# A gated delta-rule scan: block inversion over 16x16 blocks, decay mask on GpSimd, SiLU taken directly

## The chip, the cores and the metric

The kernel runs on one core of a Trainium2 chip. The time is the device time of one execution in microseconds (us); beside it stands one execution recorded by the hardware profiler. The engines are named as in the profile: PE (TensorE, with its weight loads as PEld), DVE (VectorE), ACT (ScalarE), POOL (GpSimd) and SP (SyncE, which only issues transfers).

## The reference

A backbone of two layers over 256 context tokens and 512 latent tokens, width 1024, in float32. Layer 0 joins a differential attention with a bidirectional gated DeltaNet; layer 1 joins a linear recurrence with windowed attention; each has a gated convolutional feed-forward part. Only the DeltaNet of layer 0 is touched. Cut to what matters:

```python
qkv = jax.nn.silu(_dwconv(qkv, conv_w))            # then q, k, v
qb = _l2norm(qb); kb = _l2norm(kb)
g = -exp(a_log) * softplus(a_raw + dt_bias); beta = sigmoid(b_raw)
# per chunk and direction
G = cumsum(g); decay = where(i >= j, exp(G_i - G_j), 0)
t_mat = where(i > j, beta_i * (k k^T) * decay, 0) + I
u = solve(t_mat, beta * v); w = solve(t_mat, beta * exp(G) * k)
v_new = u - w s;  o = (q exp(G)) s + (q k^T * decay) v_new
s = s * exp(G_last) + (k exp(G_last - G))^T v_new
```

## The kernel before

**Layout.** Activations lie with features on the 128 partitions and all 768 tokens on the free axis. The kernel is written in a tile framework: the program gives the work in order, and a planner, working from its own cost estimates, lays down before the run the order in which each engine executes its instructions, puts in the semaphores and shares buffers. Each engine then runs its queue strictly in that order.

**Projections.** `proj` loads one 1024x128 weight tile, splits it into a rounded high part (ACT, L333) and a low remainder (L335, two in three on DVE, one on POOL) and runs 48 matmuls of 128x384 for it (L346, L347, L349), called `pj` in the rows. Two PSUM accumulators hold them in turn.

**q and k.** `gdn_proj` adds a four-tap convolution (one ACT copy, six DVE instructions, L435) and the SiLU as y(1 + tanh(y/2)), which is twice the SiLU: a tanh on ACT (L964) and a product on DVE (L965). The factor 2 is taken out later. `gdn_qk` squares the result on ACT (L983), sums squares by a matmul with ones (L986), copies them out (L987), and forms the inverse root by Ln and Exp over all four heads at once. v goes the same way (`gdn_v`), with a transpose instead of the norm.

**The scan.** There are 6 chunks of 128 tokens and 8 problems (4 heads in 2 directions) in each. For chunk s, four functions:

- `gdn_prep`: two transfers put the rows of G across all partitions (tile A); eight DVE instructions subtract the column of G plus log-beta and add the causal mask (L804); one Exp over 128x1024 (L805); k k^T (L811) times it gives LT (L812); the four 32x32 diagonal blocks of LT are copied by ACT into LTd (L816); q k^T (L821) is multiplied onto A (L823).
- `gdn_inv`: the 32x32 diagonal blocks are inverted on DVE. A transpose spreads LTd (L831); then for each row i from 1 to 31 a product (L839) and a reduce (L840), each needing the row before; two transposes (L842, L844) give the inverse Xd and its transpose XTd.
- `gdn_merge`: two doubling levels on TensorE (L862, L869, L871, then L880, L885), with copies by ACT and DVE between, join the 32x32 inverses into 64x64 and 128x128 ones.
- `gdn_step`: applies the inverse to v, forms the output and updates the state (L903 to L952). L903 is POOL's product of q with exp(G), and L1046 are POOL's issues of loads for the attention that follows.

**Order.** k, then q, then `gdn_prep` of chunks 0 and 1 and `gdn_inv` of chunk 0, then v, then per chunk s: merge(s), step(s), prep(s+2), inv(s+1); then the attention's q, k and v projections. The planner pulls the latter forward into TensorE's gaps. 24 rows of the modulation weights, each a POOL product (L519), an ACT sum (L520) and a DVE product with sum (L525), are spread over the same time.

Of the kernel before, what the change touches and what calls it, by code (L numbers as in the profile page):

```python
# [9 lines left out]
F32 = mybir.dt.float32  # L10
# [3 lines left out]
ALU = mybir.AluOpType  # L14
# [44 lines left out]


for _n, _w in (("ident", 128), ("trif", 128), ("trir", 128), ("jrev", 128), ("mbf", 128), ("mbr", 128), ("xinit", 256),
               ("cos", 512), ("sin", 512), ("eps", 1), ("lnq", 1), ("lnk", 1), ("ones", 128)):
    _regc(_n, _w)


def _consts():
    c = np.zeros((P, _NCN), np.float32)

    def put(n, v):
        o, w = _CN[n]  # L70
# [28 lines left out]
    put("lnq", -0.5 * math.log(128.0) - math.log(2.0))  # L99
    put("lnk", -math.log(2.0))  # L100
    put("ones", 1.0)
    return c

# [140 lines left out]
class K:  # L244
# [473 lines left out]
    def gdn_scalars(self, ps):  # L718
# [67 lines left out]
    def gdn_init(self):  # L786
        nc, gp = self.nc, self.gp
        self.S = [gp.tile([P, 4, P], F32, name=f"S{d}") for d in range(2)]
        self.XT = gp.tile([P, 8, P], F32, name="XT")
        self.X64 = gp.tile([64, 8, 64], F32, name="X64")  # L790
        nc.gpsimd.memset(self.XT.rearrange("p n t -> p (n t)"), 0.0)
        nc.gpsimd.memset(self.X64.rearrange("p n t -> p (n t)"), 0.0)

    def gdn_prep(self, s):
        nc, gp = self.nc, self.gp
# [4 lines left out]
        kr = gp.tile([P, 4, P], F32, tag="kr", name=self.nm("kr"), bufs=2)  # L800
        nc.scalar.activation(kr, self.loc(kT, 1), AF.Copy)
        kk = lambda n: kT[:, n, self.chunk(0)] if n < 4 else kr[:, n - 4, :]
        for n in range(8):
            nc.vector.scalar_tensor_tensor(A[:, n, :], A[:, n, :], self.col(self.Gb, n), self.c("mbf"), op0=ALU.subtract, op1=ALU.add)  # L804
        nc.scalar.activation(A, A, AF.Exp)  # L805
        LT = gp.tile([P, 8, P], F32, tag="LT", name=self.nm("LT"), bufs=2)
        fl = lambda t: t.rearrange("p h t -> p (h t)")
        for d in range(2):
# [18 lines left out]
    def gdn_inv(self, s):  # L827
        nc, gp = self.nc, self.gp
        LTd = self.Ll.pop(s)
        Ll = gp.tile([P, 32, 32], F32, tag="Ll", name=self.nm("Ll"), bufs=1)  # L830
        nc.vector.transpose(Ll, LTd.rearrange("p n i -> p i n").unsqueeze(3).to_broadcast([P, 32, 8, 4]))  # L831
        nc.vector.memset(Ll.rearrange("p a b -> p (a b)")[:, 0:1024:33], 1.0)
        Xl = gp.tile([P, 8, 32], F32, tag="Xl", name=self.nm("Xl"), bufs=1)
        nc.gpsimd.tensor_copy(Xl.rearrange("p a b -> p (a b)"), self.c("xinit"))
        pr = gp.tile([P, 8, 32], F32, tag="pr", name=self.nm("pr"), bufs=1)
        for i in range(1, 32):
            n1, n2 = i // 4 + 1, i + 1
            lb = Ll[:, i, 0:n2].unsqueeze(1).to_broadcast([P, n1, n2])
            nc.vector.tensor_tensor(pr[:, 0:n1, 0:n2], Xl[:, 0:n1, 0:n2], lb, op=ALU.mult)  # L839
            nc.vector.tensor_reduce(Xl[:, 0:n1, i], pr[:, 0:n1, 0:n2], axis=AX.X, op=ALU.add)  # L840
        Xd = gp.tile([P, 8, 32], F32, tag="Xd", name=self.nm("Xd"), bufs=2)
        nc.vector.transpose(Xd.rearrange("p n (a g) -> p a n g", g=4), Xl)  # L842
        XTd = gp.tile([P, 8, 32], F32, tag="XTd", name=self.nm("XTd"), bufs=2)
        nc.vector.transpose(XTd, Xd)  # L844
        self.U[s] += (Xd, XTd)

    def gdn_merge(self, s):
        nc, gp = self.nc, self.gp
        blk = lambda b: slice(32 * b, 32 * b + 32)
        LT, Xd, XTd = self.U[s][3:]  # L850
        XT, X64 = self.XT, self.X64
        for b in range(4):
            nc.scalar.activation(XT[blk(b), :, blk(b)], XTd[blk(b)], AF.Copy)
        for b in range(2):
            nc.scalar.activation(X64[blk(b), :, blk(b)], Xd[blk(b)], AF.Copy)
        pa = self.gs("lv1a")
        pa3 = pa.rearrange("p (q n i) -> p q n i", q=2, i=32)
        Y = gp.tile([P, 8, 32], F32, tag="Y", name=self.nm("Y"), bufs=1)
        for p in range(2):
# [6 lines left out]
        for p in range(2):
            fr, to = 2 * p, 2 * p + 1
            for n in range(8):
                nc.tensor.matmul(pb3[blk(fr), 0, n, :], Y[blk(to), n, :], XTd[blk(to), n, :], start=True, stop=True)  # L869
# [194 lines left out]
    def layer0_mixer(self):  # L1064
        nc, tc = self.nc, self.tc
        w0 = self.ap["w0"]
        with ExitStack() as es:
# [4 lines left out]
            with self.psum("ps0", big=2, sml=PSML, gs=4 - PSML):  # L1072
# [10 lines left out]
                    A, B = self.AB(0, 0, "nm0")  # L1083
                    u = self.modulate(xs, A, B, r, us=self.useg(self.sp), mp=MPOOL[0])
                with tc.tile_pool(name="gp", bufs=1, reuse_waits="tile") as self.gp:
                    for tag, shape, n in (("kd", [P, 8, P], 1), ("Ll", [P, 32, 32], 1), ("LTd", [P, 8, 32], 1), ("Xl", [P, 8, 32], 1),
                                          ("pr", [P, 8, 32], 1), ("LT", [P, 8, P], 2)):
# [9 lines left out]
                    self.gdn_qk(4, self.kT, self.c("lnk"), u)  # L1097
# [405 lines left out]
```

## Time and profile before

| | us |
|---|---|
| median of 3 runs | 1988.56 (1987.25 to 1989.88) |
| profiled execution | 1991.65 |
| its span, first to last instruction | 1989.8 |

| engine | busy us | share of the span |
|---|---|---|
| PE | 1816.7 | 91% |
| DVE | 1306.8 | 66% |
| ACT | 879.9 | 44% |
| POOL | 513.8 | 26% |

Busy times are sums over one execution; matmuls are pipelined and their ends are modelled, so a busy PE need not be at its peak. The mean granted clock of PE over the span is 0.95 of full speed. The changed functions run between about 97 and 505 us of the span.

### The profile page before, as it was taken

Reading aid. Unit: us, or ns where it says so; the run is one execution under the profiler, and the core shown is the slowest. Engines: PE = TensorE matmul, PEld = TensorE weight load, DVE = VectorE, ACT = ScalarE, POOL = GpSimd, SP = SyncE. Lnnn points to the kernel's source line nnn. Section 1 sums busy time; section 2 is a strip of 40 time slices with the busy share of each in tenths; the row PEclk is TensorE's granted clock in tenths of the full one; section 3 lists DMA queues with packets and bytes.
Section 4 is the critical chain, followed back from the end, with each engine's and each line's share of the span. In section 5 each row is a group of like instructions: output and inputs, shape, how many; then the busy total and the mean of one; then the engine's idle time right before and its main releaser. Section 6 shows DMA issues by size and latency. Waiting matters only on the chain. (4 is left out here: it accounts for less than half of the span.)

```text
span 1989.8 us, 27199 instructions
## 1 busy us (share of the span) xinstructions
PE 1816.7 (91%) x10129; PEld 1585.1 (80%) x10129; DVE 1306.8 (66%) x2462; ACT 879.9 (44%) x1638; POOL 513.8 (26%) x376
## 2 busy tenths in 40 slices
PE   7678899889898889999999999979888999999997
PEld 2467788888786678999999999967665788888887
DVE  4898787987457566665755454677666775555556
ACT  4345543443446355432333232365666564333344
POOL 1545311221232123212223222132222331111112
PEclk9788888999889999999999999989999999999998
DMA  8433232222533123323344434224000232333323
GB/s 317 135 118 109 80 103 91 88 86 61 109 85 107 43 90 123 117 91 112 129 136 132 133 112 143 78 92 111 20 24 19 84 121 85 109 99 99 90 79 118
DMA packets 75669, 202.87 MB, mean 102 GB/s; under 512 B 8545, under 2 KB 18961, under 8 KB 75153
## 3 DMA queue, kind: packets, MB, share of 16 engines
q1 hardware_dynamic: 65984, 173.01, 27.5%
q0 software_dynamic: 4800, 11.28, 2.7%
q10 hardware_dynamic: 4752, 16.85, 2.6%
q8 instruction: 80, 1.31, 0.3%
q14 instruction: 53, 0.43, 0.1%
HBM read 189.28 MB, written 9.99 MB: 100 GB/s over the span
## 5 line engine op out<-in xcount | busy, mean ns | idle before, releaser
L333 ACT ACTIVATE hi<-raw 128x512 fp32r<-128x512 f32 (+2 forms) x429 | 262.4, 617 | 445.6 <-PE pj L347 177.0
L346 PE MATMUL pj<-uh,hi 128*128 128x384 f32 (+1 forms) x1184 | 413.3, 349 | 16.6 <-DVE cv L435 11.9
L347 PE MATMUL pj<-ul,hi 128*128 128x384 f32 (+1 forms) x1184 | 411.9, 348 | 0.0
L335 POOL TENSOR_TENSOR lo<-raw,hi 128x512 fp32r<-128x512 f32 (+1 forms) x143 | 193.6, 1354 | 717.9 <-ACT hi L333 671.1
L349 PE MATMUL pj<-uh,lo 128*128 128x384 f32 (+1 forms) x1184 | 327.1, 350 | 1.6 <-POOL lo L335 0.8
L335 DVE TENSOR_TENSOR lo<-raw,hi 128x512 fp32r<-128x512 f32 (+2 forms) x286 | 210.8, 740 | 149.3 <-ACT hi L333 142.8
L346 PEld LDWEIGHTS pj<-uh,hi 128*128 128x128 f32 x1184 | 229.6, 194 | 22.1 <-issue 15.8
L347 PEld LDWEIGHTS pj<-ul,hi 128*128 128x128 f32 x1184 | 229.6, 194 | 3.2 <-issue 0.8
L349 PEld LDWEIGHTS pj<-uh,lo 128*128 128x128 f32 x1184 | 221.0, 194 | 7.0 <-POOL lo L335 1.5
L435 DVE SCALAR_TENSOR_TENSOR y<-pj,smt,y 128x511 f32<-128x511 f32 (+1 forms) x264 | 161.6, 654 | 59.1 <-ACT y L425 56.8
L346 PE MATMUL dn<-h,hi 128*128 128x384 f32 (+2 forms) x560 | 192.8, 344 | 2.7 <-ACT hi L333 2.2
L347 PE MATMUL dn<-l,hi 128*128 128x384 f32 (+2 forms) x560 | 192.2, 343 | 0.0
L349 PE MATMUL dn<-h,lo 128*128 128x384 f32 (+2 forms) x560 | 167.7, 343 | 1.5 <-DVE lo L335 1.2
L560 DVE SCALAR_TENSOR_TENSOR x<-dn,mod,x 128x512 f32<-128x512 f32 (+1 forms) x152 | 93.0, 633 | 87.7 <-PE dn L349 87.6
L346 PE MATMUL pj<-u,hi 128*128 128x512 f32 x336 | 130.7, 389 | 0.0
L347 PE MATMUL pj<-u,hi 128*128 128x512 f32 x336 | 130.7, 389 | 0.0
L349 PE MATMUL pj<-u,lo 128*128 128x512 f32 x336 | 130.7, 389 | 0.0
L520 ACT ACTIVATE srow<-srow 128x1024 f32<-128x1024 f32 x56 | 59.3, 1058 | 153.8 <-POOL srow L519 149.0
L519 POOL TENSOR_TENSOR srow<-ada1w,srow 128x1024 f32<-128x1024 f32 x32 | 78.6, 2455 | 175.8 <-DMA ada1w<-in_ada 133.7
L346 PEld LDWEIGHTS dn<-h,hi 128*128 128x128 f32 x560 | 105.5, 188 | 10.5 <-ACT hi L333 3.6
L347 PEld LDWEIGHTS dn<-l,hi 128*128 128x128 f32 x560 | 105.4, 188 | 7.0 <-issue 0.5
L349 PEld LDWEIGHTS dn<-h,lo 128*128 128x128 f32 x560 | 103.2, 188 | 9.2 <-DVE lo L335 1.8
(423 smaller groups left out, 3447.0 us busy)
## 6 DMA issues: line engine op xcount, KB each, us to landing
raw<-in_wu SPq DMA_DIRECT2D x88, 512.0 KB, 3.6
ada1w<-in_ada SPq DMA_DIRECT2D x48, 512.0 KB, 3.7
raw<-in_w SPq DMA_DIRECT2D x38, 512.0 KB, 3.7
raw<-in_wd SPq DMA_DIRECT2D x72, 256.0 KB, 2.7
adaw<-in_ada0t ACTq DMA_DIRECT2D x24, 512.0 KB, 3.7
qk<-qdr POOLq DMA_DIRECT2D x48, 192.0 KB, 4.7
adaw<-in_ada SPq DMA_DIRECT2D x16, 512.0 KB, 7.7
raw<-in_w0o SPq DMA_DIRECT2D x16, 512.0 KB, 3.7
```

The lines of the kernel that those rows point to most:

```text
L333: nc.scalar.activation(hi, raw[:, a:b], AF.Copy)
L335: eng.tensor_tensor(lo, raw[:, a:b], hi.bitcast(F32), op=ALU.subtract)
L346: nc.tensor.matmul(ps, hi[n], xh[:, a:b], start=n == 0, stop=False)
L347: nc.tensor.matmul(ps, hi[n], xl[:, a:b], start=False, stop=False)
L349: nc.tensor.matmul(ps, lo[n], xh[:, a:b], start=False, stop=n == last)
L435: nc.vector.scalar_tensor_tensor(y[:, o0:o1], ps[:, o0 + s:o1 + s], taps[i], y[:, o0:o1], op0=ALU.mult, op1=ALU.add)
L519: nc.gpsimd.tensor_tensor(junk, raw, self.srow[:, 0, :], op=ALU.mult)
L520: nc.scalar.activation(junk, junk, AF.Copy, accum_out=col(0))
L560: nc.vector.scalar_tensor_tensor(xs[m][:, a:b], ps[:, a:b], self.mod[l][0 if a >= NC else 1][:, 8 * mi + m:8 * mi + m + 1], xs[m][:, a:b], ...
```

## The change

For q and k the SiLU is now one ACT instruction, and the constants that took the factor 2 out are adjusted (`lnq`, no bias for k, scale 1.0); v keeps the tanh form. In `gdn_prep` the mask is added to A by one POOL instruction over 128x1024, and the subtraction of the column goes into eight Exp instructions as their bias (a new small tile nGb holds its negative). In `gdn_inv` the row recurrence runs over two 16x16 blocks of each 32x32 block side by side, so i goes from 1 to 15; the off-diagonal 16x16 part is then made by two products on TensorE, 32 matmuls each, issued in turn over the four groups of 32 partitions, with an ACT copy between and a DVE add after; a tile LTo, zero but for the off-diagonal part of LTd, feeds the first. In `gdn_merge` the two halves of the first level are issued in turn instead of one after the other.

```diff
-            nc.vector.scalar_tensor_tensor(A[:, n, :], A[:, n, :], self.col(self.Gb, n), self.c("mbf"), op0=ALU.subtract, op1=ALU.add)
-        nc.scalar.activation(A, A, AF.Exp)
+        nc.gpsimd.tensor_tensor(A, A, self.c("mbf").unsqueeze(1).to_broadcast([P, 8, P]), op=ALU.add)
+        for n in range(8):
+            nc.scalar.activation(A[:, n, :], A[:, n, :], AF.Exp, bias=self.col(self.nGb, n))
...
+        nc.scalar.activation(LTo[:, :, 16:32], LTd[:, :, 16:32], AF.Copy, scale=self.c("toph"))
...
-        for i in range(1, 32):
+        X = Xl.rearrange("p (s x) -> p s x", s=2)[:, :, 0:128].rearrange("p s (a j) -> p s a j", j=32)
+        L = Ll.rearrange("p (s x) -> p s x", s=2)
+        for i in range(1, 16):
             n1, n2 = i // 4 + 1, i + 1
-            lb = Ll[:, i, 0:n2].unsqueeze(1).to_broadcast([P, n1, n2])
-            nc.vector.tensor_tensor(pr[:, 0:n1, 0:n2], Xl[:, 0:n1, 0:n2], lb, op=ALU.mult)
-            nc.vector.tensor_reduce(Xl[:, 0:n1, i], pr[:, 0:n1, 0:n2], axis=AX.X, op=ALU.add)
+            lb = L[:, :, 32 * i:32 * i + n2].unsqueeze(2).to_broadcast([P, 2, n1, n2])
+            nc.vector.tensor_tensor(pr[:, :, 0:n1, 0:n2], X[:, :, 0:n1, 0:n2], lb, op=ALU.mult)
+            nc.vector.tensor_reduce(X[:, :, 0:n1, i], pr[:, :, 0:n1, 0:n2], axis=AX.X, op=ALU.add)
...
+        nc.vector.transpose(XTd, Xd)
+        py = self.gs("lv0")
...
+        for n in range(8):
+            for b in range(4):
+                nc.tensor.matmul(py3[blk(b), n, :], LTo[blk(b), n, :], Xd[blk(b), n, 0:16], start=True, stop=True)
+        nc.scalar.activation(Y0, py3, AF.Copy)
+        for n in range(8):
+            for b in range(4):
+                nc.tensor.matmul(po3[blk(b), n, :], XTd[blk(b), n, :], Y0[blk(b), n, :], start=True, stop=True)
+        nc.vector.tensor_tensor(Xd[:, :, 0:16], Xd[:, :, 0:16], po3, op=ALU.add)
         nc.vector.transpose(XTd, Xd)
...
-        for p in range(2):
-            fr, to = 2 * p, 2 * p + 1
-            for n in range(8):
-                nc.tensor.matmul(pa3[blk(to), 0, n, :], LT[blk(fr), n, blk(to)], Xd[blk(fr), n, :], start=True, stop=True)
-            nc.scalar.activation(Y[blk(to)], pa3[blk(to), 0], AF.Copy)
+        pr = tuple((blk(2 * p), blk(2 * p + 1)) for p in range(2))
+        for n in range(8):
+            for fr, to in pr:
+                nc.tensor.matmul(pa3[to, 0, n, :], LT[fr, n, to], Xd[fr, n, :], start=True, stop=True)
+        for fr, to in pr:
+            nc.scalar.activation(Y[to], pa3[to, 0], AF.Copy)
...
-        self.tanh_silu2(y)
+        if silu:
+            nc.scalar.activation(y, y, AF.Silu)
+        else:
+            self.tanh_silu2(y)
```

## Rows read from the trace of the kernel before

**Rows 1.** Busy us (instructions) by stretch: PE, PEld, DVE, ACT, POOL; PEclk, DMA.
```profile
97.00:222.00 125.00, 98.33 (x462) 88.39 (x462) 105.66 (x152) 69.36 (x93) 64.59 (x26) 0.87 0.35 113
222.00:505.00 283.00, 256.58 (x2016) 236.73 (x2016) 229.64 (x629) 113.02 (x224) 65.28 (x57) 0.89 0.28 87
...
452.00:485.00 33.00, 30.20 (x285) 27.22 (x283) 28.91 (x92) 13.84 (x30) 6.01 (x6) 1.00 0.23 72
```

**Rows 2.** Waits of PE, 97 to 222 us: total us, times, longest.
```profile
PE l L986 <- ACT lsq L983: 17.2, 6, 4.3
PE pj L346 <- DVE cv L435: 11.9, 4, 8.4
```

**Rows 3.** Groups by line, DVE, 97 to 222 us: count, busy us, mean ns, idle.
```profile
L965 DVE SCALAR_TENSOR_TENSOR cv<-th,cv 128x768 f32<-128x768 f32 x8 | 15.1, 1891 | 1.2 <-ACT th L964 1.2
...
L804 DVE SCALAR_TENSOR_TENSOR A<-A,Gb,cst 128x128 f32<-128x128 f32 x16 | 8.7, 605 | 0.0
```

**Rows 4.** Instructions of tile Xl: min/median/max ns, first and last start.
```profile
L842 DVE STREAM_TRANSPOSE Xd<-Xl x6: 401/402/445, 273.6 to 484.5; 128x256 f32<-128x256 f32 x6
```

**Rows 5.** Waits of PE, 222 to 505 us.
```profile
PE lv1a L862 <- DVE Xd L842: 16.3, 6, 3.6
PE qk L821 <- DVE LT L812: 4.6, 4, 2.0
```

**Rows 6.** Timeline of PE, 269 to 276 us: start, length.
```profile
269.56 0.33 PE L346 MATMUL pj<-uh,hi 128*128 128x384 f32 x1
269.73 0.33 PE L347 MATMUL pj<-ul,hi 128*128 128x384 f32 x1
...
274.07 1.05 PE L862 MATMUL lv1a<-Xd,LT 32*32 32x32 f32 x16 [3.65 <-DVE Xd L842]
...
275.54 0.52 PE L347 MATMUL pj<-ul,hi 128*128 128x384 f32 x1
275.86 0.52 PE L346 MATMUL pj<-uh,hi 128*128 128x384 f32 x1
```

**Rows 7.** Groups by line, DVE, whole span.
```profile
L839 DVE TENSOR_TENSOR pr<-Xl,Ll 128x2 f32<-128x2 f32 (+30 forms) x186 | 71.4, 384 | 4.8
...
L840 DVE TENSOR_REDUCE Xl<-pr 128x1 f32<-128x2 f32 (+30 forms) x186 | 47.3, 254 | 4.8
...
L804 DVE SCALAR_TENSOR_TENSOR A<-A,Gb,cst 128x128 f32<-128x128 f32 x48 | 17.6, 432 | 4.4 <-DMA A<-gdr 4.4
```

**Rows 8.** Groups by line and shape, DVE, 222 to 505 us.
```profile
L839 DVE TENSOR_TENSOR pr<-Xl,Ll 128x196 f32<-128x196 f32 x6 | 6.0, 1006 | 0.1
...
L840 DVE TENSOR_REDUCE Xl<-pr 128x6 f32<-128x126 f32 x6 | 1.7, 281 | 0.1
...
L840 DVE TENSOR_REDUCE Xl<-pr 128x4 f32<-128x64 f32 x6 | 1.3, 220 | 0.2
...
L840 DVE TENSOR_REDUCE Xl<-pr 128x1 f32<-128x4 f32 x6 | 0.9, 154 | 0.2
```

**Rows 9.** Timeline of PE, 455 to 459 us, between two merge levels.
```profile
455.83 0.21 PE L869 MATMUL lv1b<-XTd,Y 32*32 32x32 f32 x1
...
456.33 0.19 PE L871 MATMUL lv1b<-Y,XTd 32*32 32x32 f32 x1
...
457.69 0.69 PE L869 MATMUL lv1b<-XTd,Y 32*32 32x32 f32 x16
```

**Rows 10.** Groups by line, ACT, whole span.
```profile
L915 ACT ACTIVATE kd<-ktok,kds 128x128 f32<-128x128 f32 x40 | 10.8, 385 | 0.5 <-PE ktok L913 0.4
...
L387 ACT ACT_TABLE_LOAD x7 | 9.0, 1283 | 0.1
...
L805 ACT ACTIVATE A<-A 128x1024 f32<-128x1024 f32 x6 | 6.3, 1048 | 4.1 <-DVE A L804 4.1
```

**Rows 11.** Groups by line, POOL, whole span.
```profile
L519 POOL TENSOR_TENSOR srow<-adaw,srow 128x1024 f32<-128x1024 f32 x24 | 64.1, 2671 | 60.6 <-ACT srow L520 41.8 <-DMA adaw<-in_ada0t 16.3 <-DVE adaw L525 1.3
```

**Rows 12.** Waits of POOL, 220 to 500 us.
```profile
POOL B L903 <- ACT B L901: 64.5, 3, 22.7
```

More of the change, by code (lines that the diff above doesn't have):

```diff
@@ L61 @@
 for _n, _w in (("ident", 128), ("trif", 128), ("trir", 128), ("jrev", 128), ("mbf", 128), ("mbr", 128), ("xinit", 256),
-               ("cos", 512), ("sin", 512), ("eps", 1), ("lnq", 1), ("lnk", 1), ("ones", 128)):
+               ("cos", 512), ("sin", 512), ("eps", 1), ("lnq", 1), ("toph", 1), ("ones", 128)):
     _regc(_n, _w)
@@ L98, in _consts @@
     put("eps", EPS)
-    put("lnq", -0.5 * math.log(128.0) - math.log(2.0))
-    put("lnk", -math.log(2.0))
+    put("lnq", -0.5 * math.log(128.0))
+    put("toph", (i % 32 < 16).astype(np.float32)[:, None])
     put("ones", 1.0)
@@ L760, in gdn_scalars @@
         nc.vector.tensor_tensor(self.Gb, G, spb, op=ALU.add)
+        self.nGb = self.small(48, "nGb")
+        nc.vector.tensor_scalar(self.nGb, self.Gb, -1.0, None, op0=ALU.mult)
         pr = self.gs("GT")
@@ L792, in gdn_init @@
         nc.gpsimd.memset(self.X64.rearrange("p n t -> p (n t)"), 0.0)
+        self.LTo = gp.tile([P, 8, 32], F32, name="LTo")
+        nc.gpsimd.memset(self.LTo.rearrange("p n t -> p (n t)"), 0.0)
     def gdn_prep(self, s):
@@ L829, in gdn_inv @@
         LTd = self.Ll.pop(s)
[L830 to L835, printed above, removed]
@@ L836, in gdn_inv @@
-        for i in range(1, 32):
+        LTo = self.LTo
+        nc.scalar.activation(LTo[:, :, 16:32], LTd[:, :, 16:32], AF.Copy, scale=self.c("toph"))
+        Ll = gp.tile([P, 1056], F32, tag="Ll", name=self.nm("Ll"), bufs=1)
+        nc.vector.transpose(Ll[:, 0:1024].rearrange("p (a b) -> p a b", b=32),
+                            LTd.rearrange("p n i -> p i n").unsqueeze(3).to_broadcast([P, 32, 8, 4]))
+        nc.vector.memset(Ll[:, 0:1024:33], 1.0)
+        Xl = gp.tile([P, 288], F32, tag="Xl", name=self.nm("Xl"), bufs=1)
@@ L837, in gdn_inv @@
+        nc.gpsimd.tensor_copy(Xl[:, 0:256], self.c("xinit"))
+        pr = gp.tile([P, 2, 4, 16], F32, tag="pr", name=self.nm("pr"), bufs=1)
+        X = Xl.rearrange("p (s x) -> p s x", s=2)[:, :, 0:128].rearrange("p s (a j) -> p s a j", j=32)
+        L = Ll.rearrange("p (s x) -> p s x", s=2)
+        for i in range(1, 16):
             n1, n2 = i // 4 + 1, i + 1
-            lb = Ll[:, i, 0:n2].unsqueeze(1).to_broadcast([P, n1, n2])
-            nc.vector.tensor_tensor(pr[:, 0:n1, 0:n2], Xl[:, 0:n1, 0:n2], lb, op=ALU.mult)
@@ L840, in gdn_inv @@
-            nc.vector.tensor_reduce(Xl[:, 0:n1, i], pr[:, 0:n1, 0:n2], axis=AX.X, op=ALU.add)
+            lb = L[:, :, 32 * i:32 * i + n2].unsqueeze(2).to_broadcast([P, 2, n1, n2])
+            nc.vector.tensor_tensor(pr[:, :, 0:n1, 0:n2], X[:, :, 0:n1, 0:n2], lb, op=ALU.mult)
+            nc.vector.tensor_reduce(X[:, :, 0:n1, i], pr[:, :, 0:n1, 0:n2], axis=AX.X, op=ALU.add)
         Xd = gp.tile([P, 8, 32], F32, tag="Xd", name=self.nm("Xd"), bufs=2)
-        nc.vector.transpose(Xd.rearrange("p n (a g) -> p a n g", g=4), Xl)
+        nc.vector.transpose(Xd.rearrange("p n (a g) -> p a n g", g=4), Xl[:, 0:256].rearrange("p (a b) -> p a b", b=32))
@@ L843, in gdn_inv @@
         XTd = gp.tile([P, 8, 32], F32, tag="XTd", name=self.nm("XTd"), bufs=2)
+        nc.vector.transpose(XTd, Xd)
+        blk = lambda b: slice(32 * b, 32 * b + 32)
+        py = self.gs("lv0")
+        py3 = py[:, 0:128].rearrange("p (n i) -> p n i", i=16)
+        po3 = py[:, 128:256].rearrange("p (n i) -> p n i", i=16)
+        Y0 = gp.tile([P, 8, 16], F32, tag="Y0", name=self.nm("Y0"), bufs=1)
+        for n in range(8):
+            for b in range(4):
+                nc.tensor.matmul(py3[blk(b), n, :], LTo[blk(b), n, :], Xd[blk(b), n, 0:16], start=True, stop=True)
@@ L858, in gdn_merge @@
         Y = gp.tile([P, 8, 32], F32, tag="Y", name=self.nm("Y"), bufs=1)
-        for p in range(2):
-            fr, to = 2 * p, 2 * p + 1
-            for n in range(8):
-                nc.tensor.matmul(pa3[blk(to), 0, n, :], LT[blk(fr), n, blk(to)], Xd[blk(fr), n, :], start=True, stop=True)
-            nc.scalar.activation(Y[blk(to)], pa3[blk(to), 0], AF.Copy)
+        pr = tuple((blk(2 * p), blk(2 * p + 1)) for p in range(2))
[4 more added lines that the diff above has]
+            nc.scalar.activation(Y[to], pa3[to, 0], AF.Copy)
         pb = self.gs("lv1b")
         pb3 = pb.rearrange("p (q n i) -> p q n i", q=2, i=32)
[L866 to L869, printed above, removed]
+        for n in range(8):
+            for p, (fr, to) in enumerate(pr):
+                nc.tensor.matmul(pb3[fr, 0, n, :], Y[to, n, :], XTd[to, n, :], start=True, stop=True)
                 if p == 0:
-                    nc.tensor.matmul(pb3[blk(to), 1, n, :], XTd[blk(to), n, :], Y[blk(to), n, :], start=True, stop=True)
-            nc.vector.tensor_copy(XT[blk(fr), :, blk(to)], pb3[blk(fr), 0])
+                    nc.tensor.matmul(pb3[to, 1, n, :], XTd[to, n, :], Y[to, n, :], start=True, stop=True)
+        for p, (fr, to) in enumerate(pr):
+            nc.vector.tensor_copy(XT[fr, :, to], pb3[fr, 0])
             if p == 0:
-                nc.vector.tensor_copy(X64[blk(to), :, 0:32], pb3[blk(to), 1])
+                nc.vector.tensor_copy(X64[to, :, 0:32], pb3[to, 1])
         lo, hi = slice(0, 64), slice(64, 128)
@@ L965, in tanh_silu2, with gdn_proj @@
         nc.vector.scalar_tensor_tensor(y if out is None else out, th, 1.0, y, op0=ALU.add, op1=ALU.mult)
-    def gdn_proj(self, j, u):
+    def gdn_proj(self, j, u, silu=True):
         nc = self.nc
@@ L988, in gdn_qk @@
         f = dst.rearrange("p h t -> p (h t)")
-        self.rstd_from(f, 4 * T, 0.25, f, lnbias=lnb)
+        self.rstd_from(f, 4 * T, 1.0, f, lnbias=lnb)
         for h in range(4):
@@ L994, in gdn_v @@
         nc = self.nc
-        y = self.gdn_proj(8 + h, u)
+        y = self.gdn_proj(8 + h, u, False)
         for g in range(2):
@@ L1085, in layer0_mixer @@
                 with tc.tile_pool(name="gp", bufs=1, reuse_waits="tile") as self.gp:
-                    for tag, shape, n in (("kd", [P, 8, P], 1), ("Ll", [P, 32, 32], 1), ("LTd", [P, 8, 32], 1), ("Xl", [P, 8, 32], 1),
-                                          ("pr", [P, 8, 32], 1), ("LT", [P, 8, P], 2)):
+                    for tag, shape, n in (("kd", [P, 8, P], 1), ("Ll", [P, 1056], 1), ("LTd", [P, 8, 32], 1), ("Xl", [P, 288], 1),
+                                          ("pr", [P, 2, 4, 16], 1), ("LT", [P, 8, P], 2)):
                         self.gp.tile(shape, F32, tag=tag, name=self.nm(tag), bufs=n)
@@ L1096, in layer0_mixer @@
                     self.a0next = 16
-                    self.gdn_qk(4, self.kT, self.c("lnk"), u)
+                    self.gdn_qk(4, self.kT, None, u)
                     self.gdn_qk(0, self.qT, self.c("lnq"), u)
```

## The prediction

> **What bounds the kernel now.** I read the busy table by stretches first. Only the first layer's mixer runs the changed lines, and there they fall into two stretches: 97 to 222 us (projections of k and q) and 222 to 505 us (v, the scan, and the attention projections that fill its gaps) [rows 1]. The reader is to see that no engine is free in them: DVE is busy 105.7 of 125 us and 229.6 of 283, TensorE 98.3 and 256.6, at a mean granted clock of 0.87 and 0.89. The clock has two levels, 1.2 and 2.4 GHz, so a mean of 0.89 over 283 us is a loss of 0.11 x 283 = 31 us of TensorE time, and 0.13 x 125 = 16 us in the first stretch.
>
> Then the waits. In the first stretch TensorE stands 17.2 us for the squares of the l2 norm and 11.9 us for the convolution to leave PSUM [rows 2]; the squares wait for DVE's SiLU product. In the second it stands 16.3 us, in six pieces of up to 3.6 us, for the inverted blocks, and 4.6 us for the masked product LT [rows 5]. Inversions follow one another on DVE: the transposes that end the six of them start from 273.6 to 484.5 us, 42 us apart [rows 4], and what follows the last one is just a merge and a step, to 505. So DVE's inversion paces the scan, and TensorE fills the gaps almost fully with projections. The order of instructions on each engine is laid down before the run: a wait that the planner did not foresee stops everything queued behind it.
>
> What TensorE must do in 222 to 505 at the full clock: 283 less 26.4 idle less 31 for the clock = 226 us. That is the floor for anything that frees DVE.
>
> **The change, part by part.** *SiLU for q and k.* Eight products go from DVE, 15.1 us, mean 1.89 us [rows 3]; the activation that was a tanh stays one activation of the same size. The chain convolution, SiLU, square, norm matmul loses that step, so of TensorE's 17.2 us I let 10 go. Against it: the decay exponentials of chunks 0 and 1 lie in the same stretch, now 16 instead of 2, and a change between them and the SiLU wants a table load of 1.28 us [rows 10] each way. I allow 4 loads more, 5 us of ACT, which was busy 69.4 of 125 [rows 1]; they cost little unless they stand ahead of a square. Bounds: 0 and 16 loads (20 us of ACT).
>
> *Mask on POOL.* 48 DVE instructions go, 17.6 us [rows 7], 16 of them with 8.7 us in the first stretch [rows 3]. POOL gets six of 128x1024; its nearest row, of the same size with two inputs, takes 2.67 us [rows 11]. The exponential of a chunk becomes eight of 128x128 with a bias column, nearest row 0.385 us each, 3.1 us against 1.05 us [rows 10]; the first product LT needs four of the eight. So LT comes some 1.2 us later per chunk if POOL is free when the decay rows land (about 2.7 for DVE's 2.2, then 1.5 for 1.05). LT matters because TensorE already waits for it [rows 5] with all queued projections behind. Four preparations lie in the scan: 4 x 1.2 = 5 us. Bounds: 0 (projections planned in between) and the queue of the second rival.
>
> Weighed with this: products of two SBUF operands on DVE stretch when POOL works; the 196-element product takes 1.006 us on average where the reduce of 126 takes 0.281 and the 4-element one 0.154 [rows 8]. The Trainium skill (SBUF — State Buffer, section "SBUF: two separate sides") says that GpSimd and a DVE instruction with two SBUF inputs lock each other out for a whole instruction. The trace agrees. By it the two early masks could hold DVE 2 x 2.67 = 5.3 us of the 8.7 they free, and the first stretch would give some 3 us less than I forecast below.
>
> *Inversion by 16x16.* Now 31 products and 31 reduces a chunk take (71.4 + 47.3) / 6 = 19.8 us [rows 7]. After, 15 of each, over two blocks at a time, with 4 to 128 elements. By size from the reduces [rows 8]: three at 0.154, four near 0.18, four near 0.22, four near 0.27, sum 3.15 us; products stretched as now (384 / 254 = 1.51) 4.75 us; 7.9 us together. Added on DVE: one more transpose and one add from PSUM, 0.4 us each by the transpose's row [rows 4]. Net 11 us a chunk, 66 in all; with the masks' other 8.9, 75 of DVE's 229.6 us go.
>
> TensorE gets 2 x 32 products of 32x32x16, two records each as now, 128 a chunk. Nearest rows: in alternation over column groups, records of 32 columns start every 15 ns (35 between 455.83 and 456.33, three lines mixed); in one group, 16 take 0.69 us, some 33 ns each after the first's 0.19 [rows 9]. Bounds 128 x 15 = 1.9 and 128 x 33 = 4.2 us a chunk, double at the low clock. I take 2.2, as the new ones go in turn over four row groups. The same turn put on the merge's two levels saves about 1.0 a chunk (the second passes of 0.6 each). Net 1.2 x 6 = 7 us. The Trainium skill (TensorE: Matmul & The Clock Gate, section "Wait — 56ns, not 53.3ns?") has starts never closer than about 25 ns however narrow the matmul. The rows show 15 ns with column groups in turn, so it does not hold here; by it the six chunks would cost 128 x 25 ns x 6 = 19 us instead of 13, 6 us more.
>
> New waits: TensorE for the inverse, for ACT's copy of the first product, and DVE for TensorE's second; behind them on each queue stand projections and weight splits. The chain of DVE work that the planner can misjudge is halved, so I give the three together 1.5 us a chunk, 9 us, for the 16.3 that go. Bounds 0 and 3.6 a chunk.
>
> *Clock.* After the 3.65 us wait the projections start 0.32 us apart, before it 0.17 [rows 6]: the wait costs as much again in speed. With waits of half the length I expect 31 us to become 20.
>
> **The sum.** First stretch: 10 from the norm waits, 3 from clock and PSUM: -13. (Half of the 24 us that leave DVE there; TensorE's floor, 125 - 27 - 16 = 82 us, is far enough down.) Second: work 226 + 7 = 233; idle 26.4 - 16.3 + 9 + 5 = 24; clock 20; together 277 against 283: -6. What follows 505 us is not touched. One more: a scan that ends before the projections lets the attention loads, now waiting for the scan's last reads, run beside them: -2. Total -21. The profiled execution took 1991.65 us with a span of 1989.8, 0.16% above the median of 1988.56, so the same difference applies: 1967.5 us.
>
> **Rivals.**
> (a) *The waits vanish.* DVE has 75 us to spare, so no inverse comes late: idle 10, clock loss 10, first stretch -18: 253 for 283, total -48, 1940.5 us. For it: from 452 to 485 the clock is full although the scan's matmuls run [rows 1]. Against it: two new hops per chunk.
> (b) *TensorE was the bound all along.* Idle stays 26, clock 31, work +7, LT +5 in the scan; the first stretch gives 13 less 4 for table loads: about +3, 1991, or with half of these 1983; I take 1985. For it: TensorE busy 91% of the stretch.
> (c) *Slower: the mask stands behind POOL's product of q.* POOL is in order, and its product for the state's output stands up to 22.7 us at the head of the queue [rows 12]. If the planner puts the next chunk's mask behind it, LT comes some 6 us late, TensorE stands behind the pending qk products for 4 x 6 = 24 us, and each such gap halves the clock afterwards, some 4 us: 16 more. It decides from a mask that starts over 2 us after its rows land. Forecast's scan +40, less the first stretch: +19, 2007.5 us. Against it: today the rows' arrival and that product nearly coincide, so either order may come.
>
> **How the numbers follow.** Forecast 0.54 (own range 1953 to 1981), (a) 0.16, (b) 0.14, (c) 0.16. 0.2%, 4 us, is what a measurement can tell from no change. Faster by more: all of the first two, half of (b), 0.77. Within: 0.08, most of the rest of (b). Slower: 0.15, (c). The range reaches from (a)'s figure, 1938, to 1994, past (b) and short of (c).
>
> **What would show it.** Right: DVE in the scan down by 70 to 80 us; the last inverse well before 484 us less 13; no wait over 2 us ahead of the first merge level; the new products 1 to 1.3 us per level; q's norm done by about 210 us. Wrong: TensorE waiting on the second products for LT more than 10 us in all, with the mask late on POOL (c); more than six further table loads before 222 us; granted clock below 0.87 in the scan; or new products at over 30 ns a record.

## The result, and the profile after

The change made the kernel 43.9 us faster, where 21 were forecast:

| | before | after |
|---|---|---|
| median us | 1989.22 (1987.25 to 1993.31, 4 runs) | 1945.34 (1940.53 to 1947.59, 4 runs) |
| ratio | | 0.9774, 95% interval 0.9748 to 0.9799 |
| profiled execution, span | 1991.65, 1989.8 | 1947.22, 1945.4 |
| busy PE, DVE, ACT, POOL | 1816.7, 1306.8, 879.9, 513.8 | 1793.1, 1217.1, 898.2, 525.4 |
| mean granted clock | 0.950 | 0.969 |

The time came out between the forecast (1967.5) and just above rival (a) (1940.5), outside the forecast's own range and inside the stated one.

The two spans differ by 44.4 us. To see where, I cut both at the same events: DVE's first final multiply of q (220.1 before, 202.5 after), the first attention scores (511.3, 471.5) and the first matmul of the output projection of the attention (657.7, 613.3). Nothing before 97 us or after the last of these moves. Busy us (instructions) by stretch, PE, PEld, DVE, ACT, POOL, then PEclk and DMA; first the kernel before:

```profile
97.00:220.10 123.10, 97.62 (x460) 88.10 (x460) 103.76 (x150) 67.51 (x90) 62.74 (x25) 0.86 0.36 114
220.10:511.30 291.20, 262.16 (x2048) 241.42 (x2047) 232.07 (x630) 117.35 (x231) 71.01 (x65) 0.89 0.30 90
511.30:657.70 146.40, 124.94 (x755) 107.77 (x753) 94.77 (x219) 73.00 (x178) 34.27 (x39) 0.91 0.31 81
```

and the changed kernel:

```profile
97.00:202.50 105.50, 87.68 (x447) 80.61 (x448) 77.28 (x118) 73.59 (x101) 58.95 (x24) 0.94 0.38 119
202.50:471.50 269.00, 248.12 (x2808) 226.02 (x2806) 167.92 (x426) 130.43 (x277) 88.03 (x73) 0.97 0.36 109
471.50:613.30 141.80, 124.99 (x776) 108.86 (x774) 95.42 (x219) 73.16 (x179) 33.56 (x37) 0.95 0.27 75
```

Length less busy PE is idle PE. The first stretch is 17.6 us shorter: 7.7 idle (25.5 to 17.8) and 9.9 busy (13 fewer matmuls lie in it, the rest is clock, 0.86 to 0.94). The second is 22.2 shorter: 8.2 idle (29.0 to 20.9) and 14.0 busy, although it holds 760 more matmuls. The third is 4.6 shorter, all of it idle.

Waits of PE after, in the second stretch (205 to 472 us; total us, times, longest), which answer to [rows 5]:

```profile
PE qk L825 <- DVE LT L816: 7.9, 4, 3.1
PE pj L346 <- DVE cv L435: 4.4, 1, 4.4
PE lv L904 <- DVE X L898: 1.7, 1, 1.7
...
PE lv L865 <- ACT Y L862: 0.7, 3, 0.3
...
PE lv1b L892 <- ACT Y L887: 0.5, 1, 0.5
```

The 16.3 us for the inverse are gone to the last one: the matmuls that use it first, L861 and L885, are not in the list. The new hop to ACT and back costs 0.7 us (L865); the merge's own copies cost 1.7 (L904) and 0.5 (L892). The wait for LT grew from 4.6 to 7.9 us, and 4.4 us stand for a convolution that has to leave PSUM, a wait that this stretch did not have before. In the first stretch (97 to 205 us, against [rows 2]):

```profile
PE pj L346 <- DVE cv L435: 15.3, 5, 8.4
PE l L1013 <- ACT lsq L1010: 5.5, 3, 2.5
```

The groups that answer to [rows 7, 9, 10] (busy us, mean ns of one | idle before):

```profile
L848 DVE TENSOR_TENSOR pr<-Xl,Ll 128x4 f32<-128x4 f32 (+14 forms) x90 | 33.5, 372 | 2.3
L849 DVE TENSOR_REDUCE Xl<-pr 128x2 f32<-128x4 f32 (+14 forms) x90 | 18.8, 209 | 2.2
L807 POOL TENSOR_TENSOR A<-A,cst 128x1024 f32<-128x1024 f32 x6 | 15.7, 2615 | 28.4 <-DMA A<-gdr 28.4
L809 ACT ACTIVATE A<-A,nGb 128x128 f32<-128x128 f32 x48 | 14.8, 389 | 11.4 <-POOL A L807 11.4
L861 PE MATMUL lv<-Xd,LTo 32*32 32x16 f32 x384 | 4.5, 182 | 0.0
L865 PE MATMUL lv<-Y,XTd 32*32 32x16 f32 x384 | 4.5, 182 | 0.7 <-ACT Y L862 0.7
L885 PE MATMUL lv1a<-Xd,LT 32*32 32x32 f32 x192 | 4.2, 192 | 0.0
```

The recurrence takes (33.5 + 18.8) / 6 = 8.7 us a chunk for 19.8; the last inverse (its transpose) starts at 400.9 instead of 484.5 us, and the last output of the scan comes at about 428 us, 43 before the first scores (505 and 511 before): the projections that used to run beside the scan now have a stretch to themselves. The new products cost 9.0 us in all.

How the mask delays LT is read from the timeline of one chunk (start, length, [idle before <- releaser]):

```profile
299.97 2.41 POOL L807 TENSOR_TENSOR A<-A,cst 128x1024 f32<-128x1024 f32 x1 [7.53 <-DMA A<-gdr]
...
302.41 2.45 ACT L809 ACTIVATE A<-A,nGb 128x128 f32<-128x128 f32 x8 [0.80 <-POOL A L807]
...
303.79 0.69 DVE L816 SCALAR_TENSOR_TENSOR LT<-kk,A 128x512 f32<-128x512 f32 x1 [6.40 <-ACT A L809]
304.53 1.16 PE L825 MATMUL qk<-qT,kr 128*128 128x128 f32 x8 [1.26 <-DVE LT L816]
```

POOL stands ready when the rows land and starts at once; then 2.4 us of mask and four Exps are 3.8 us to LT, with DVE idle for 6.4 us and TensorE at the end of the chain.

### The profile page after: what moved, and what is told of

It reads as the page before. It is cut to its first block, busy times and chain, and to the rows that moved or that the text cites. A ratio compares the mean times of both kernels' runs of the same rounds, so it can differ in the third digit from the quotient of the medians.

```text
span 1945.4 us, 28578 instructions
## 1 busy us (share of the span) xinstructions
PE 1793.1 (92%) x10897; PEld 1563.7 (80%) x10897; DVE 1217.1 (63%) x2227; ACT 898.2 (46%) x1697; POOL 525.4 (27%) x383
## 5 line engine op out<-in xcount | busy, mean ns | idle before, releaser
L349 PE MATMUL pj<-uh,lo 128*128 128x384 f32 (+1 forms) x1184 | 322.4, 346 | 1.9 <-DVE lo L335 1.1
L349 PEld LDWEIGHTS pj<-uh,lo 128*128 128x128 f32 x1184 | 217.1, 191 | 7.3 <-POOL lo L335 1.8
```

Of the source, the lines that this page charges most:

```text
L349: nc.tensor.matmul(ps, lo[n], xh[:, a:b], start=False, stop=n == last)
```

## The experiments

Three parts are told apart: S (SiLU direct), M (mask on POOL, eight Exps), I (16x16 inversion with its products and the merge's turn). Each run carries its ratio to the kernel before on its own chip. That kernel's median lay between 1988 and 1997 us on these chips, and the intervals are 0.3 to 0.5% to either side, so differences below 8 us between chips are weak. On the chip of e1 to e4 it took 1996.88 us: by the ratios these four gain 29, 20, 50 and 37 us, where their medians against 1989 say 24, 12, 43 and 31.

**e1: S alone.** Edit:

```diff
-        self.tanh_silu2(y)
+        nc.scalar.activation(y, y, AF.Silu)   # q and k only
```

> The kernel before with the direct SiLU for q and k as its only change. Theory A (each part acts in its own stretch: the SiLU shortens the stretch up to q's norm, the inversion the scan): the multiply that ends q's norm starts near 204 instead of 220 us, TensorE's wait for the squares falls from 17.2 to about 6 us, the waits for the inverse stay near 16 us, and the time is 12 to 16 us below before: about 1975. Theory B (any DVE time removed is worth the same, 44 us for the 90 us of DVE that the whole change removed, so 0.49 us each): 15 us of DVE give 7 us: 1982. Theory C (the SiLU carries nearly everything, since the scan is bound by TensorE): 30 us or more: 1959.

Measured 1964.76 (1963.15 to 1975.49), ratio 0.9856 (0.9810 to 0.9901). q's multiply starts at 198.9 us. More than A and B allowed, and by the ratio near the 30 of C, whose reason e3 takes away. From 97 us to q's multiply it is 21.2 us shorter than before; the whole change, which has M's Exps in the same stretch, is 17.6 shorter. The waits for the inverse fell too, to 11.3 us in four, though no inversion changed. It gets only an earlier start.

```profile
PE lv1a L861 <- DVE Xd L841: 11.3, 4, 4.3
```

**e2: M alone.** Edit:

```diff
-            nc.vector.scalar_tensor_tensor(A[:, n, :], ..., self.c("mbf"), ...)
-        nc.scalar.activation(A, A, AF.Exp)
+        nc.gpsimd.tensor_tensor(A, A, self.c("mbf")..., op=ALU.add)
+            nc.scalar.activation(A[:, n, :], A[:, n, :], AF.Exp, bias=self.col(self.nGb, n))
```

> The kernel before with the decay mask on POOL and eight Exps with a bias as its only change. Theory A: DVE loses 17.6 us, but TensorE's wait for LT grows from 4.6 to some 8 us and table loads are added before 222 us: between 5 us faster and 3 us slower, about 1988. Theory B: 17.6 us of DVE at 0.49 give 9 us: 1980. Theory C: no change within 4 us.

Measured 1977.47 (1971.30 to 1978.92), ratio 0.9898 (0.9849 to 0.9946). LT's waits grew to 12.3 us, the inverse's fell to 9.1 (the second and third row together). B was nearest; A missed.

```profile
PE qk L823 <- DVE LT L814: 12.3, 4, 4.2
PE lv1a L864 <- DVE Xd L844: 7.1, 3, 3.7
...
PE lv1a L864 <- DVE Ll L834: 2.0, 2, 1.2
```

**e3: I alone.** Edit, with the products and the turn behind it:

```diff
-        for i in range(1, 32):
+        for i in range(1, 16):
```

> The kernel before with the 16x16 inversion, its two products and the merge's turn as its only change. Theory A: TensorE's wait for the inverse goes from 16.3 to under 2 us, the granted clock of the scan's stretch rises from 0.89 to about 0.95, the stretch up to q's norm stays as before (multiply at 220 us), and the time is 22 to 30 us below before: about 1963. Theory B: DVE loses about 63 us, 31 us at 0.49: 1958. Theory C (the scan is bound by TensorE, which gets 7 us more work): 1985 or more.

Measured 1946.24 (1944.25 to 1946.87), ratio 0.9750 (0.9712 to 0.9787): as much as the whole change gains, from one part. Its scan against the changed kernel's and before's, the window from q's multiply to the first scores, and its waits for LT:

```profile
219.00:472.80 253.80, 241.94 (x2795) 220.54 (x2793) 165.35 (x450) 120.45 (x242) 69.03 (x66) 0.99 0.37 109
```

```profile
PE qk L824 <- DVE LT L815: 2.3, 4, 0.9
```

It starts 16.5 us later than the changed kernel and ends 1.3 later: 11.9 us idle for 20.9, clock 0.99 for 0.97. C fell, and so did A and B, which gave this part 1963 and 1958.

**e4: S and M, no I.** Edit against the change:

```diff
-        for i in range(1, 16):
+        for i in range(1, 32):
```

> The changed kernel with the 32x32 inversion and the merge order of before: SiLU and mask alone. Theory A: 12 to 18 us below before, about 1974, with six waits for the inverse as before (some 16 us) and a clock near 0.89 in the scan. Theory B: 32.7 us of DVE at 0.49 give 16 us: 1973 (this run does not tell A from B). Theory C: 40 us below before, 1950.

Measured 1958.28 (1956.31 to 1960.36), ratio 0.9812 (0.9773 to 0.9850). Faster than A and B said (1974, 1973), and by the ratio, 37 us, near the 40 of C. The inverse's waits are down to 6.3 us in three, where A had six as before, and LT's are up to 10.9:

```profile
PE qk L822 <- DVE LT L813: 10.9, 4, 3.3
PE lv1a L863 <- DVE Xd L843: 6.3, 3, 4.6
```

**e5 (S and I), e6 (M and I).** Edits against the change, e5 then e6:

```diff
-        nc.gpsimd.tensor_tensor(A, A, self.c("mbf")..., op=ALU.add)
+            nc.vector.scalar_tensor_tensor(A[:, n, :], ..., self.c("mbf"), ...)
...
-            nc.scalar.activation(y, y, AF.Silu)
+            self.tanh_silu2(y)
```

> The changed kernel with the decay mask back on DVE and one Exp: SiLU and inversion together. Theory D (the mask costs time in the scan: with it TensorE waits 7.9 us for LT and idles 9 us more over the scan than in the inversion-only kernel, which gives away the 17 us that the SiLU gains): the multiply of q starts near 199 us, the waits for LT fall to some 2 us, the first attention scores start near 455 instead of 471.5 us, and the time is 1928 to 1933. Theory E (the start of the attention is pinned near 472 us by the total of TensorE's work, whatever DVE is spared): 1943 to 1947, first scores at 469 to 472.

> The changed kernel with the tanh form for q and k: mask and inversion together. Theory D: it has the mask's cost without the SiLU's gain: first scores near 484 us and a time of 1953 to 1960. Theory E: scores near 472, 1943 to 1947, since the inversion alone reaches that too.

e5: 1938.47 (1936.92 to 1940.96), ratio 0.9710 (0.9673 to 0.9746). e6: 1960.14 (1955.46 to 1965.44), ratio 0.9818 (0.9776 to 0.9860). With e1 to e4 this makes a table of medians, from several chips:

| us | tanh form | SiLU direct |
|---|---|---|
| 32x32, mask on DVE | 1989 | 1965 |
| 32x32, mask on POOL | 1977 | 1958 |
| 16x16, mask on DVE | 1946 | 1938 |
| 16x16, mask on POOL | 1960 | 1945 |

The mask on POOL helps while DVE's inversions pace the scan and costs once they don't: 12 and 6 us faster in the table's 32x32 rows, 14 and 7 slower in the 16x16 rows (20 and 9, 14 and 13 by the ratios). e6 waits 9.3 us for LT where e3 waits 2.3:

```profile
PE qk L826 <- DVE LT L817: 9.3, 4, 4.0
```

E is refuted by e6: its first scores come at 488.7 us, not near 472, and it does not end where e3 does. e5 ends earlier than E said, but its first scores, at 467.0, are only 2 us before E's 469 to 472. D's sign is right, but its size for e5 was too large by 5 to 10 us: of the 19 us by which S starts the scan earlier, 8 are left.

**e7, e15: the change without the merge's turn.** Edit, in each of the two loops:

```diff
-        for n in range(8):
-            for fr, to in pr:
+        for p in range(2):
+            for n in range(8):
```

> The changed kernel with the merge's first level in the order of before, one half after the other. The forecast had the turn save 1.0 us of TensorE time a chunk. Theory D (TensorE is full in the scan, so its time counts): 4 to 8 us slower than the changed kernel, 1950 to 1953, and the records of the first level cost as before (10.3, 11.1 and 5.6 us for the three lines). Theory E' (the merge lies beside DVE's work): within 2 us of it, 1944 to 1947.

> The changed kernel without the merge's turn, beside it on one chip. If the turn saves what the first level's groups fell by (10.3 to 4.2 us in one line, some 1 us a chunk): 4 to 8 us slower than the changed kernel. If the halves overlapped with other matmuls anyway: within 3 us.

e7: 1950.65 (1941.99 to 1959.85), too wide to tell. e15, beside the changed kernel (e13) on one chip: 1948.03 (1944.87 to 1954.32) against 1942.30 (1938.65 to 1947.17), slower in 19 of 20 pairs of runs; that is within the 4 to 8 us of the first case, but the two ratios, 0.9787 and 0.9762, have overlapping intervals. The first level's groups in e15:

```profile
L885 PE MATMUL lv1a<-Xd,LT 32*32 32x32 f32 x192 | 8.2, 192 | 0.4 <-ACT Y L886 0.4
L892 PE MATMUL lv1b<-XTd,Y 32*32 32x32 f32 x192 | 8.2, 192 | 0.0
...
L894 PE MATMUL lv1b<-Y,XTd 32*32 32x32 f32 x96 | 4.1, 192 | 0.0
```

Together 20.5 us, against 4.2 + 5.6 + 5.2 = 15.0 with the turn: 0.9 us a chunk, as forecast. The rest of the fall from 27.0 before goes with the clock: a record of these lines took 213 to 222 ns on average there and takes 192 here.

**e8: as e5, the Exp in two halves.** Edit:

```diff
-        nc.scalar.activation(A, A, AF.Exp)
+            if n % 4 == 3:
+                nc.scalar.activation(A[:, n - 3:n + 1, :], A[:, n - 3:n + 1, :], AF.Exp)
```

> As e5, but the Exp of a chunk in two halves of 128x512, each after its four DVE instructions, so that the first product LT waits for half of the work. Theory D: LT comes some 1.5 us earlier in each of four chunks; at most 2 to 4 us faster than e5, about 1927. Theory E: as e5, 1943 to 1947.

Measured 1939.79 (1934.80 to 1942.12): no gain over e5 that shows; LT's waits are 5.1 us there, 3.8 in e5.

**e9: as e3, the recurrence run twice.** Edit:

```diff
+        for rep in range(2):
+            if rep:
+                nc.gpsimd.tensor_copy(Xl[:, 0:256], self.c("xinit"))
             for i in range(1, 16):
```

> The inversion-only kernel with its row recurrence run twice (the tile set back between), so that DVE's chain ahead of the inverse is again about as long as before (some 8 us more a chunk, 48 in all) while TensorE's work and everything else stays. Theory D (the long DVE chain made TensorE late and cost its clock; the shorter one is the gain): waits for the inverse return, some 8 to 16 us, idle and clock loss from q's norm to the first scores go from 14 us back to some 40, and the time is about 1970. Theory F (the gain comes from the new order of the work, not from the chain's length): within 5 us of the inversion-only kernel's 1946.

Measured 1972.58 (1968.94 to 1974.88), ratio 0.9893 (0.9839 to 0.9947), as D said. TensorE's work is that of e3; its scan (window, then the waits of PE in it):

```profile
218.40:501.80 283.40, 260.30 (x2793) 235.50 (x2793) 205.32 (x630) 120.42 (x242) 74.23 (x72) 0.91 0.33 95
```

```profile
PE qk L824 <- DVE LT L815: 6.5, 4, 2.2
PE lv L863 <- DVE Xd L853: 4.8, 2, 2.9
```

Against e3 the scan is 29.6 us longer: 11.2 more idle and 18.4 more busy for the same matmuls, at clock 0.91 for 0.99. F is refuted. The inverse is late by some 5 us in all rather than 8 to 16, and LT by 4.2 more than in e3; for each us of idle that came back, 1.6 were lost in speed.

**e10, e11: as e3, the new products left out, or issued twice.** Edit of e10 (the lines from L861 to the second transpose), then of e11 (likewise for L865):

```diff
-                nc.tensor.matmul(py3[blk(b), n, :], LTo[blk(b), n, :], Xd[blk(b), n, 0:16], start=True, stop=True)
...
+                nc.tensor.matmul(py3[blk(b), n, :], LTo[blk(b), n, :], Xd[blk(b), n, 0:16], start=True, stop=True)
```

> The inversion-only kernel without the two products of the off-diagonal 16x16 part, their copies, the add and the second transpose (that part of the inverse is left out). Theory D (TensorE is full in the scan at the full clock, so its work counts one for one): 768 matmuls go that took 9 us by their groups; 7 to 13 us faster, 1933 to 1939. Theory G (the products lie in gaps): within 3 us of 1946.

> The inversion-only kernel with each of the new 32x32x16 products issued twice. Theory D: 768 more matmuls at the price of e10: 7 to 13 us slower, 1953 to 1959. Theory G: within 3 us of 1946.

e10: 1938.88 (1933.32 to 1945.45), ratio 0.9729 (0.9676 to 0.9782), 7.4 us below e3 on another chip. That is D's figure, but the ratios overlap (4 us apart), so the medians don't rule out G. For D speaks the profiled execution: its scan takes 245.0 us, 8.8 less than e3's, for 9 us of products, though that execution (1933.42 us) is one of the two fast ones of four. e11: 1978.34 (1970.95 to 1981.68), ratio 0.9933 (0.9905 to 0.9962), 32 us above e3 where 7 to 13 were expected. Where the other 20 went, in windows of 2 us behind the doubled products of one chunk:

```profile
326.00:328.00 2.00, 2.00 (x126) 1.66 (x114) 1.65 (x3) 1.64 (x5) 0.00 (x0) 1.00 0.03 8
328.00:330.00 2.00, 1.03 (x86) 0.98 (x83) 1.70 (x6) 0.16 (x1) 0.94 (x1) 0.93 0.27 59
330.00:332.00 2.00, 2.00 (x9) 1.78 (x6) 1.45 (x6) 0.83 (x2) 0.83 (x1) 0.50 0.58 211
...
344.00:346.00 2.00, 2.00 (x6) 0.87 (x5) 1.53 (x5) 0.00 (x0) 0.00 (x0) 0.50 0.00 0
...
348.00:350.00 2.00, 2.00 (x18) 1.84 (x17) 1.57 (x6) 1.79 (x6) 0.00 (x0) 1.00 0.00 0
```

After the burst of narrow matmuls, which has one gap of 0.97 us that the trace lays to no releaser, TensorE runs for some 16 us at 1.2 GHz while it is busy throughout. Such gaps ("issue" in the waits of PE) add up to 8.4 us in seven pieces over e11's scan; e3 has none, and e11's idle time there is 18.8 us for 11.9:

```profile
PE lv L865 <- issue: 3.4, 3, 1.4
...
PE lv1a L886 <- issue: 2.1, 1, 2.1
PE lv L866 <- issue: 1.9, 2, 1.0
...
PE pj L348 <- issue: 1.0, 1, 1.0
```

The clock falls behind six of the seven. And a burst need not be doubled for it: in e14 (the next group), whose products are issued once, the profiled execution has one such gap of 1.43 us within a product, and behind it some 14 us at 1.2 GHz with TensorE busy throughout (the gap from the timeline, then windows of 2 us):

```profile
338.73 0.30 PE L865 MATMUL lv<-Y,XTd 32*32 32x16 f32 x11 [1.43 <-issue]
```

```profile
342.00:344.00 2.00, 2.00 (x47) 1.61 (x48) 0.40 (x1) 0.88 (x3) 0.00 (x0) 0.50 0.00 0
...
352.00:354.00 2.00, 2.00 (x7) 1.28 (x6) 1.73 (x8) 0.60 (x1) 0.00 (x0) 0.50 0.00 0
```

e8 has a gap of 1.31 us in the same product, with the clock down for only some 3 us behind it.

**e12, e14, e16: the mask as DVE's addition, eight Exps kept (e16: in two halves).** Edit:

```diff
-        nc.gpsimd.tensor_tensor(A, A, self.c("mbf")..., op=ALU.add)
+        nc.vector.tensor_tensor(A, A, self.c("mbf")..., op=ALU.add)
```

> The changed kernel with the mask as one DVE addition of 128x1024 instead of POOL's, the eight Exps with a bias kept. If POOL's 2.4 us are what makes LT late: the waits for LT fall from 7.9 to some 4 us and the time to that of e5, 1936 to 1940. If the eight Exps (2.45 us against 1.05) and their table loads in the first stretch are: LT's waits stay near 7 us and the time near 1946.

> The changed kernel itself, as the base for the other three on the same chip: 1945 by its first timing (ratio 0.977).

> The mask as one DVE addition, eight Exps kept, beside the changed kernel on one chip. If POOL's mask costs what the first runs suggest (it makes LT late by 1.2 us and TensorE is the bound): 6 to 10 us faster than the changed kernel. If that difference was the chips': within 3 us of it.

> As e14, the DVE addition in two halves of 128x512, each followed by its four Exps, so that the first product LT waits for half of the mask. If LT's arrival counts: 1 to 4 us faster than e14. If TensorE has other work there: within 2 us.

e12: 1937.65 (1933.66 to 1945.83), LT's waits 4.9 us. On one chip: e13 1942.30, e14 1937.14 (1928.34 to 1942.25), e16 1938.89 (1936.84 to 1940.13). e14 and e16 are faster than e13 in 45 of 50 pairs of runs, by 5.2 and 3.4 us at the medians, between the 3 and the 6 that were to tell; their ratios, 0.9723 (0.9686 to 0.9761) and 0.9736 (0.9695 to 0.9778), overlap e13's 0.9762 (0.9720 to 0.9804). POOL's instruction, not the eight Exps, makes up most of LT's delay: with the Exps kept, its waits are 4.9 us in e12 and 4.7 in e14, against 7.9 and 7.2 in the two executions of the change. The halves cut these waits to 2.5 us and bring no time that shows. So the best version found is the change with the mask on DVE, in any of the forms of e5, e8, e14 and e16 (1937 to 1940, which these runs do not order); it is likely 3 to 7 us below the change, an effect at the edge of what was measured.

## Why the prediction was wrong

The direction was right, and so was the mechanism of the main terms; the size was half. The step that failed is the price of TensorE's waits in the scan: 9 us of new waits were put for the 16.3 that go, and from them follows the clock, "With waits of half the length I expect 31 us to become 20". The runs showed 0.7 us of new waits in the new hops, and a clock loss of 8 us where 20 was expected. "3 from clock and PSUM" in the first stretch was too small as well. By the prediction's own terms:

| | forecast | measured |
|---|---|---|
| first stretch | -13 | -17.6 |
| second: new work | +7 | +3.5 (9.0 added, 5.5 saved by the turn) |
| second: idle | -2 | -8.2 |
| second: clock | -11 | -17.5 (busy -14.0, less +3.5) |
| attention begins sooner | -2 | -4.6 (all idle) |
| total | -21 | -44.4 |

- **The clock.** I priced the wait that goes at the average of before, one us of clock for one of idle. What counts is the margin: e9 gives 1.6 us of lost speed for each us of idle put back, and between before and after it is about 2 (17.5 for 8.2). Counted as the forecast counts, the missing share of PEclk times the length, the 31 us became 0.03 x 269 = 8; the -17.5 of the table is what is left of the busy time. When the waits for the inverse go altogether, most of the loss goes: e3 has 0.01 x 254 = 2.5 us left by PEclk. That is rival (a)'s "clock loss 10", which I gave 0.16, and its -18 for the first stretch came out too; what it had wrong is the idle time, 20.9 us for its 10.
- **Idle.** I put 9 us of new waits for the 16.3 that go, because the planner might misjudge the new hops. In the new hops they came to 0.7 us. Unforeseen were 4.4 us for a convolution and 1.7 for the merge's second level. The allowance of 5 us for LT was fair (7.9 less 4.6 is 3.3), though its own figures, 2.7 + 1.5 less 2.2 + 1.05, give 0.95 us a chunk and not 1.2.
- **First stretch.** The waits for the squares gave 11.7 us for the 10 said, the wait for PSUM grew by 3.4 (and the 4.4 in the second stretch) instead of falling, and five more table loads came (four allowed). The busy time gave 9.9: some 2 us are the 13 matmuls moved out, the rest clock.
- **The inversion on DVE** was sized well: 8.7 us a chunk for 7.9; DVE's load fell by 64.2 us in the second stretch (75 said) and 89.7 in all.
- **New products** take 0.73 us a level where I expected 1 to 1.3; the turn 0.9 for 1.0. That they count nearly in full, because the scan had become TensorE's, is what e10's profile says and its medians leave open.
- **Rival (c)** did not happen: the four masks of the scan find POOL idle and start when their rows land (28.4 us of idle before them, all laid to that transfer). The loss it foresaw is there in a milder form, 2.4 us of POOL in the chain to LT.
- **The attention.** That its loads would run beside the projections is not what the 4.6 us show: the wait that got shorter is that of its scores for their Exp.
- **That parts add up** was assumed throughout and is wrong. S, M and I alone give about 24, 12 and 43 us against 1989 (29, 20 and 50 by the ratios), and together 44: all three shorten the same waits for the inverse (16.3 us before; 11.3, 9.1 and none), and once I has removed them, S is worth 8 to 15 and M less than nothing. Of the forecast's sum, the first stretch's 13 was therefore partly the same time as the second's. This alone would have made the gain smaller than the forecast; the terms above outweighed it.
- **A slip in the range:** its lower end, 1938, is called (a)'s figure, which is 1940.5.

**The two places where a page was weighed.** Beside a POOL instruction a recurrence product of 32 elements, whose neighbours take 0.2 us, lasts as long as that instruction (changed kernel, timeline):

```profile
314.32 1.83 POOL L1060 TENSOR_TENSOR aq<-aq,ah 128x768 fp32r<-128x768 f32 x1 [2.79 <-DVE Xl L849]
314.35 1.84 DVE L848 TENSOR_TENSOR pr<-Xl,Ll 128x32 f32<-128x32 f32 x1
```

The lock of which the Trainium skill speaks (SBUF — State Buffer, section "SBUF: two separate sides") agrees with these two rows. The price that was worked out from it for the two early masks, up to 5.3 us of DVE, came to some 2: beside them one DVE instruction takes 3.37 us, where the same one takes 1.23 with POOL idle.

```profile
100.49 1.23 DVE L525 SCALAR_TENSOR_TENSOR adaw<-adaw,srow 128x1024 f32<-128x1024 f32 x1
...
104.57 5.67 POOL L807 TENSOR_TENSOR A<-A,cst 128x1024 f32<-128x1024 f32 x2
104.65 3.37 DVE L525 SCALAR_TENSOR_TENSOR adaw<-adaw,srow 128x1024 f32<-128x1024 f32 x1 [2.92 <-POOL srow L519]
```

With row groups in turn, the 64 records of one level lie in 0.73 us (changed kernel, timeline of PE), (0.73 - 0.18) / 63 = 8.7 ns from start to start:

```profile
272.97 0.73 PE L861 MATMUL lv<-Xd,LTo 32*32 32x16 f32 x64
```

The floor of some 25 ns in the Trainium skill (TensorE: Matmul & The Clock Gate, section "Wait — 56ns, not 53.3ns?") does not hold for these rows, and the measurement decides.

**What stays open.** Why S's 19 us of earlier start are worth only 8 beside I: e5 ends its last inversion where e3 does (397.3 and 396.1 us), with 16.9 us of idle for 11.9, and no single wait carries the difference. Why the attention's first part is 4.6 us shorter: its scores wait 2.3 us for their Exp instead of 6.9 (before, then after), but no run isolates the cause.

```profile
L634 PE MATMUL scp<-qk,qk 128*128 128x256 f32 (+1 forms) x80 | 30.7, 395 | 6.9 <-ACT e L638 6.9
```

```profile
L634 PE MATMUL scp<-qk,qk 128*128 128x256 f32 (+1 forms) x80 | 29.8, 384 | 2.4 <-ACT e L638 2.3
```

And what holds the clock down in e11. Doubled products are not needed for it, as e14 shows; the gaps stand ahead of both falls, but no run puts in a gap by itself, and what makes the gaps is not known.

## What to carry to other kernels

Price a wait on TensorE with the speed that is lost behind it, by the margin and not the average: here 1.6 to 2 us for each us of idle, from two comparisons. Edits that relieve the same chain don't add up; forecast the largest first, and then ask of each other one whether its engine still bounds: moving work to an idle engine (the mask) pays while the old engine paces and costs by its latency afterwards. Small matmuls issued in turn over row and column groups are cheap (0.73 us for 64 records), but look for gaps in their stream: in e11 and e14 the clock fell behind such gaps.

## What the runs showed of the hardware

- Bursts of 32x32x16 matmuls with a gap of 0.97 us (e11, products doubled) or 1.43 us (e14, products issued once) that the trace lays to no releaser were followed by 16 and 14 us at 1.2 GHz with TensorE busy, a gap of 1.31 us (e8) by some 3; e3, with single bursts and no such gap, kept a mean clock of 0.99 in its scan. e11 lost 32 us by 768 matmuls whose first set takes 9.
- 11.2 us of idle time put back into e3's scan (e9) came with 18.4 us more of busy time for the same matmuls, at a mean clock of 0.91 for 0.99.
- Records of 32x32x16 matmuls issued in turn over the four groups of 32 partitions start 8.7 ns apart (64 in 0.73 us).
- A DVE product of 32 elements, 0.2 us otherwise, took 1.84 us beside a POOL instruction of 1.83 us.
- Two executions of the changed kernel, 1947.22 and 1938.65 us, differ by 8.6 us. Of this, 6.7 us lie between 97 us and the output projection: TensorE's idle time there is 55.5 and 54.1 us, and the other 5.3 us are busy time for the same work, at a mean clock of 0.96 and 0.97. So even here part of the spread between executions (and perhaps between chips) is the clock.
